# Weight loads issued from GpSimd, ScalarE's stores from ScalarE, and GpSimd's arithmetic on other engines

## The chip, the cores and the metric

The kernel runs on one core of a Trainium2 chip, as one launch. The metric is the device time of that launch in microseconds, the median of several runs. A core has a matrix engine (TensorE, PE), a vector engine (VectorE, DVE), an activation engine (ScalarE, ACT), a general engine (GpSimd, POOL) and a queue engine (SyncE, SP). Each has its own instruction stream and works in order; semaphores tie the streams together. A DMA is issued by an instruction in one of these streams: if that instruction must wait, everything behind it in the stream waits too.

## The reference

A trunk of two layers over 512 latent tokens and 256 context tokens, 1024 channels, one batch entry, all in float32. Cut to what matters:

```python
for l in range(DEPTH):                                   # DEPTH = 2
    mod = silu(c) @ w_mod[l] + b_mod[l]                  # shifts, scales, gates; the same for the context
    h = modulate(rmsnorm(x, g0), shift1, scale1)
    s5, q, k, v, hq, hff, hfb, hi, hg, gate = split_columns(h @ w_in[l])
    ya = s5_branch(s5)                    # bidirectional diagonal state space model, then a GLU
    yb = windowed_attention(rope(q), rope(k), v)         # window 128, context keys, sink logits
    yc = hgrn2_branch(hq, hff, hfb, hi, hg)              # gated linear recurrence, both directions
    m = sum(sigmoid(gate_b) * (y_b @ w_branch[b]) for b, y_b in enumerate((ya, yb, yc)))
    x = x + g1 * rmsnorm(m @ w_out[l], g1n)
    h = modulate(rmsnorm(x, g2n), shift2, scale2)
    a, g = split(depthwise_conv(h @ w_up[l]))
    x = x + g2 * rmsnorm((silu(a) * g) @ w_down[l], g3n)
# the context stream goes through the same layer, except in the last; the latent stream is returned
```

## The kernel before

**Weights.** Channels lie on partitions and tokens along the free axis (tiles of 128x768: 256 context and 512 latent columns). Every weight tile of 128x1024 is split into a high and a low part. `wload` (L286) loads it into a raw buffer `wr` (three buffers), ScalarE rounds it to `wh`, VectorE subtracts to get `wl`; `product` (L312) then makes three matmuls per 128 channels (high by high, high by low, low by high). The results go to PSUM in `mm` (512 columns, two buffers) and `mc` (256 columns, one buffer), and ScalarE or VectorE evacuates them. `hold` (L335) does the same with weights that stay in SBUF for a while, as the down projection does.

**Stages.** A layer runs: norm and `s5_in` (L1421, the s5 branch's columns of `w_in`, evacuated by ScalarE and stored to DRAM in eight stores `ud` a tile); attention (`att_in` L1018 with its rotary helper `rope`, `attention` L1065, whose result goes to `yb`); `hgrn` (L1280) with its input `hg_in` (L1231, which stores the output gate `tgd`), woven with `gates` (L854, which stores the branch gates `gd`) and with set-up work; `s5` (L1715, with `stage_a` and `stage_b`, which stores `yd`), `merge`, `w_out`, `residual` (L584), `ffn` (L732). The norms' last step is `norm_part` (L552): TensorE transposes pieces into PSUM (`pa`), ScalarE applies scale and shift, GpSimd makes the rounded high part and VectorE the low part.

**Set-up work.** `mods_rows` (L418) makes modulation vectors from loads of `in_wmodt` by VectorE; `s5_prep` (L1655) makes the s5 branch's matrices and passes them through DRAM: `mid`, `bbd`, `cad` in, `mt` (stored from a tile that ScalarE wrote), `kd` and `tod` out. `stage_a` loads `mt`, `tod`, `cad` and `phd` back.

**Order.** A scheduler that builds the program decides the order of each engine's instructions by priorities: weight loads are raised (`high_priority`), set-up is lowered. Scratch tiles come from one pool of 52 slots, so a tile's name says little: `slot` may be any of them. All DMAs are SyncE's. DMAs of SyncE and ScalarE take turns on eight completion counters (`DMAHW0` to `DMAHW7` in the rows of the order), and each waits for the one eight before it; GpSimd's have eight of their own (`DMASW0` to `DMASW7`). Every instruction is recorded through one helper, so each row of the profile names L121: tiles tell the rows apart.

## Time and profile before

| | us |
|---|---|
| median of three runs (lowest, highest) | 2694.89 (2693.42, 2697.78) |
| the profiled execution | 2701.07 |
| its span, first to last instruction | 2699.3 |
| TensorE's matmuls busy | 2536.5 |
| VectorE, ScalarE, GpSimd busy | 1896.8, 1021.7, 121.0 |

The mean granted clock of TensorE over the span is 0.975 of full speed. Times of the profile are from one execution and start at its first instruction. A row of a timeline gives the start, the length and the instructions that follow each other alike (x4), and in brackets the engine's idle time before them and what ended it; SPq is SyncE as a queue, where the length is that of issuing. A releaser is inferred from semaphores: the last thing that the instruction waited for.

### The profile page before, as it was taken

What the parts mean: (1) busy time and instruction counts of PE and PEld (TensorE: products, weight loads), DVE (VectorE), ACT (ScalarE), POOL (GpSimd) and SP (SyncE); (2) the same over time, 40 slices, a digit from 0 to 9 for tenths busy, and PEclk for the clock granted to TensorE, in tenths of its full rate; (3) what the DMA queues carried; (4) which work ended last, traced back from release to release, by engine and by line L of the source; (5) the groups of instructions that cost most, each with busy time, mean ns of one, the idle gap of its engine ahead of it and who ended that gap; (6) DMA issues with size and microseconds to landing.
All of it is one profiled execution on the core that took longest, in us unless ns stands there. A gap on an engine that the chain in (4) does not pass through costs nothing. (4 is left out here: it accounts for less than half of the span.)

```text
span 2699.3 us, 47069 instructions
## 1 busy us (share of the span) xinstructions
PE 2536.5 (94%) x18436; PEld 2129.6 (79%) x18436; DVE 1896.8 (70%) x4304; ACT 1021.7 (38%) x1813; POOL 121.0 (4%) x182
## 2 busy tenths in 40 slices
PE   5999998899989999999999989899999989999998
PEld 3876776687878898887888878667787778888887
DVE  6799483778576659999974566754767856666656
ACT  3356522221223345442433463562222334443334
POOL 1100000001000010000000011000000000100000
PEclk8999999999989999999999999999999989999999
DMA  7443545453566344534434557422334565333332
GB/s 246 129 127 118 166 146 164 156 165 99 169 210 213 119 128 145 162 108 131 123 102 123 155 180 222 130 82 93 107 116 131 170 213 167 110 121 112 96 100 96
DMA packets 243214, 381.36 MB, mean 141 GB/s; under 512 B 54032, under 2 KB 139440, under 8 KB 242992
## 3 DMA queue, kind: packets, MB, share of 16 engines
q1 hardware_dynamic: 242992, 378.36, 44.8%
q8 instruction: 145, 2.38, 0.4%
q14 instruction: 77, 0.63, 0.1%
HBM read 301.26 MB, written 81.21 MB: 142 GB/s over the span
## 5 line engine op out<-in xcount | busy, mean ns | idle before, releaser
L121 PE MATMUL mm<-slot,wh 128*128 128x512 f32 (+1 forms) x3798 | 1200.3, 394 | 23.5 <-DVE slot L121 9.4
L121 PEld LDWEIGHTS mm<-slot,wh 128*128 128x128 f32 x3798 | 699.8, 190 | 160.9 <-DVE slot L121 13.4
L121 PE MATMUL mm<-slot,wl 128*128 128x512 f32 (+1 forms) x1899 | 742.3, 391 | 2.7 <-issue 1.9
L121 DVE TENSOR_TENSOR slot<-slot,slot 128x384 f32<-128x384 f32 (+17 forms) x1340 | 666.3, 535 | 101.5 <-ACT slot L121 59.3
L121 PE MATMUL mc<-slot,wh 128*128 128x256 f32 (+1 forms) x3082 | 666.7, 309 | 9.4 <-ACT slot L121 7.3
L121 PEld LDWEIGHTS mc<-slot,wh 128*128 128x128 f32 x3082 | 518.8, 193 | 57.2 <-ACT slot L121 10.8
L121 DVE TENSOR_TENSOR wl<-wr,wh 128x1024 fp32r<-128x1024 f32 (+1 forms) x274 | 333.8, 1219 | 239.3 <-ACT wh L121 235.1
L121 ACT ACTIVATE wh<-wr 128x1024 fp32r<-128x1024 f32 (+1 forms) x274 | 288.5, 1053 | 531.3 <-PE mc L121 373.0
L121 PE MATMUL mc<-slot,wl 128*128 128x256 f32 (+1 forms) x1541 | 474.6, 308 | 0.0
L121 PEld LDWEIGHTS mm<-slot,wl 128*128 128x128 f32 x1899 | 359.9, 190 | 72.8 <-DVE wl L121 1.6
L121 PEld LDWEIGHTS pa<-slot,slot 128*32 128x32 f32 (+2 forms) x5696 | 213.2, 133 | 126.5 <-issue 62.3
L121 PE MATMUL pa<-slot,slot 128*32 128x32 f32 (+8 forms) x5696 | 254.8, 227 | 57.8 <-DVE slot L121 26.5
L121 PEld LDWEIGHTS mc<-slot,wl 128*128 128x128 f32 x1541 | 296.7, 193 | 14.1 <-issue 1.2
L121 ACT ACTIVATE slot<-slot 128x768 fp32r<-128x768 f32 (+5 forms) x253 | 168.3, 669 | 367.8 <-DVE slot L121 307.7
L121 ACT ACTIVATE slot<-mm 128x512 f32<-128x512 f32 (+1 forms) x180 | 103.6, 576 | 320.7 <-PE mm L121 299.5
L121 DVE CUSTOM_DVE_ANT_0 mscr<-slot,slot 128x768 bf16<-128x768 f32 (+1 forms) x256 | 178.2, 696 | 41.0 <-DMA slot<-in_wmodt 37.5
L121 ACT ACTIVATE slot<-pa 128x512 f32<-128x512 f32 (+7 forms) x250 | 115.3, 493 | 231.0 <-PE pa L121 189.8
L121 PE MATMUL pa<-cst,slot 128*128 128x128 f32 x900 | 139.5, 286 | 23.8 <-DVE slot L121 13.2
L121 PEld LDWEIGHTS pa<-cst,slot 128*128 128x128 f32 x900 | 107.4, 145 | 53.2 <-ACT slot L121 23.4
L121 PE MATMUL mm<-slot,slot 128*128 128x256 f32 (+1 forms) x784 | 111.1, 319 | 17.4 <-DMA slot<-in_wmod 15.6
L121 DVE SCALAR_TENSOR_TENSOR slot<-slot,slot 128x256 f32<-128x256 f32 (+7 forms) x129 | 92.3, 722 | 41.0 <-ACT slot L121 40.3
L121 PEld LDWEIGHTS mm<-slot,slot 128*128 128x128 f32 (+1 forms) x784 | 93.1, 185 | 22.6 <-issue 17.9
(160 smaller groups left out, 1521.9 us busy)
## 6 DMA issues: line engine op xcount, KB each, us to landing
wr<-in_win SPq DMA_DIRECT2D x108, 512.0 KB
wr<-in_wup SPq DMA_DIRECT2D x88, 512.0 KB
slot<-in_wmodt SPq DMA_DIRECT2D x80, 384.0 KB
wr<-in_wdn SPq DMA_DIRECT2D x32, 512.0 KB
slot<-cad SPq DMA_DIRECT2D x48, 256.0 KB
wr<-in_wbr SPq DMA_DIRECT2D x24, 512.0 KB
slot<-in_wmodt SPq DMA_DIRECT2D x80, 128.0 KB
cad<-slot SPq DMA_DIRECT2D x64, 144.0 KB
```

Source lines behind the costliest of these rows:

```text
L121: return _f(*(x.ap if isinstance(x, Slot) else x for x in a), **{k: x.ap if isinstance(x, Slot) else x for k, x in kw.items()})
```

## The change

The 288 weight loads of `wload` and `hold` are issued by GpSimd. The 162 stores of tiles that ScalarE has just written (`gd` 48, `yb` 10, `tgd` 8, `ud` 64, `mt` 32) are issued by ScalarE. The other 935 DMAs stay with SyncE. GpSimd computes nothing: in `norm_part` ScalarE writes the high part from PSUM itself, and VectorE computes the unrounded value from PSUM once more and subtracts; the rotary product goes to VectorE, the gate's key `k` to ScalarE, the memsets to VectorE, and the scan mask is one ScalarE copy of a broadcast.

```diff
         with self.tc.high_priority(offset=self.whp):
-            nc.sync.dma_start(raw[:, :n], src)
+            nc.gpsimd.dma_start(raw[:, :n], src)
...
             with self.tc.high_priority(offset=self.whp):
-                nc.sync.dma_start(raw[:, :P * n], src)
+                nc.gpsimd.dma_start(raw[:, :P * n], src)
...
-                nc.scalar.activation(h[:, tk], pt[:, n * i:n * i + n], AF.Identity,
-                                     bias=self.mod[l][:, 8 * sh + k, tt:tt + 1],
-                                     scale=self.amod[l][:, j, k, tt:tt + 1])
-                nc.gpsimd.tensor_scalar(hh[:, tk], h[:, tk], 1.0, 0.0, ALU.mult, ALU.add)
+                a, b = self.amod[l][:, j, k, tt:tt + 1], self.mod[l][:, 8 * sh + k, tt:tt + 1]
+                nc.scalar.activation(hh[:, tk], pt[:, n * i:n * i + n], AF.Identity, bias=b, scale=a)
+                nc.vector.tensor_scalar(h[:, tk], pt[:, n * i:n * i + n], a, b, ALU.mult, ALU.add)
                 nc.vector.tensor_sub(hl[:, tk], h[:, tk], hh[:, tk].bitcast(F32))
...
-                nc.sync.dma_start(d[:, t0:], tg[:, t0:])
+                nc.scalar.dma_start(d[:, t0:], tg[:, t0:])
...
-            nc.gpsimd.tensor_mul(s[:, 256:], s[:, 256:], sin)
+            nc.vector.tensor_mul(s[:, 256:], s[:, 256:], sin)
...
-            nc.gpsimd.tensor_scalar(k, th, self.hgn[:, c:c + 1], self.hgc[:, c:c + 1], ALU.mult, ALU.add)
+            nc.scalar.activation(k, th, AF.Identity, bias=self.hgc[:, c:c + 1], scale=self.hgn[:, c:c + 1])
...
-                nc.sync.dma_start(d[16 * j:16 * j + 16].rearrange("c g k -> g c k"), u[:, 96 * j:96 * j + 96])
+                nc.scalar.dma_start(d[16 * j:16 * j + 16].rearrange("c g k -> g c k"), u[:, 96 * j:96 * j + 96])
...
-            nc.gpsimd.memset(bb, 0.0)
+            nc.vector.memset(bb, 0.0)
...
-            nc.gpsimd.memset(mz, 1.0)
-            nc.gpsimd.tensor_mul(m3, m3, m8k[:, x0:x0 + 4].unsqueeze(2).to_broadcast([P, 4, 96]))
-            nc.gpsimd.memset(m3[:, :, 0:1], 0.0)
+            nc.scalar.activation(m3, m8k[:, x0:x0 + 4].unsqueeze(2).to_broadcast([P, 4, 96]), AF.Copy)
+            v.memset(m3[:, :, 0:1], 0.0)
```

The other stores of the list change in the same way, and one more memset goes to VectorE.

The scheduler moves much with it. Three places, first SyncE while the first layer's `hgrn` runs with set-up behind it; before, with `wr` the weights' raw buffers:

```order
L121 DMA slot_764_4679<-mid_1225 128x512
L121 DMA mt_4672<-slot_766_4686 128x512
L121 DMA mt_4672<-slot_768_4694 128x512
L121 DMA tod_4663<-kd_4366 8x16x128 x3
L121 DMA wr_5901<-in_win 128x1024
L121 DMA tod_4663<-kd_4366 8x16x128
L121 DMA wr_6110<-in_win 128x1024
L121 DMA tod_4663<-kd_4366 8x16x128 x4
L121 DMA slot_769_4697<-in_wmodt 128x768
L121 DMA slot_771_4705<-in_wmodt 128x768
```

and in the change:

```order
L121 DMA slot_764_4679<-mid_1225 128x512
L121 DMA slot_769_4697<-in_wmodt 128x768
L121 DMA tod_4663<-kd_4366 8x16x128 x8
L121 DMA slot_771_4705<-in_wmodt 128x768
L121 DMA slot_770_4704<-in_wmodt 128x256
L121 DMA slot_772_4712<-in_wmodt 128x768
L121 DMA slot_770_4704<-in_wmodt 128x256
L121 DMA slot_800_5009<-bbd_1231 128x2x128
L121 DMA slot_809_5044<-in_wmodt 128x768
```

The weight loads are gone, the `tod` stores stand in one piece, and an `in_wmodt` load stands ahead of them. Second SyncE in the first layer's `s5` stage, before (`mt` is loaded for the next products, `yd` is stored for the merge):

```order
L121 DMA yd_8432<-slot_1189_8426 16x8x96
L121 DMA wr_9046<-in_wglu 128x1024
L121 DMA yd_8432<-slot_1189_8426 16x8x96 x7
L121 DMA gd_8500<-slot_1196_8497 128x768
L121 DMA slot_1198_8502<-mt_5333 128x768
L121 DMA slot_1199_8504<-mt_5333 128x256
L121 DMA slot_1200_8506<-phd_1230 128x768
```

and in the change (`slot_1198` and `slot_1199` are the same two loads of `mt`):

```order
L121 DMA slot_1198_8496<-mt_5333 128x768
L121 DMA slot_1207_8544<-yd_1397 128x768
L121 DMA slot_1185_8390<-mt_5333 128x256
L121 DMA slot_1186_8392<-phd_1230 128x768
L121 DMA slot_1210_8550<-yd_1397 128x768
L121 DMA yd_7965<-slot_1127_7959 16x8x96 x8
L121 DMA slot_1183_8386<-ud_853 128x768
L121 DMA slot_1199_8498<-mt_5333 128x256
L121 DMA slot_1200_8500<-phd_1230 128x768
```

Both `mt` loads now stand ahead of the eight `yd` stores of the same tile, which follow eleven rows below (`yd_8426`), though the second stands behind the stores of the tile before; no weight load is near. Third ScalarE in the first layer's `s5_in`, before (`mm` and `mc` are evacuations from PSUM):

```order
L121 ACTIVATE slot_140_550<-mm_500 128x8x64
L121 ACTIVATE wh_795<-wr_794 128x1024
L121 ACTIVATE slot_140_550<-mc_501 128x8x32
L121 ACTIVATE slot_166_690<-mm_640 128x8x64
L121 ACTIVATE wh_877<-wr_876 128x1024
L121 ACTIVATE slot_166_690<-mc_641 128x8x32
L121 ACTIVATE slot_178_776<-mm_726 128x8x64
```

and in the change, with what each instruction waits for in brackets:

```order
L121 ACTIVATE slot_140_550<-mc_501 128x8x32 [waits PE_49]
L121 DMA ud_553<-slot_140_550 8x16x96 [waits DMAHW2_49,Activation_49]
L121 DMA ud_553<-slot_140_550 8x16x96 [waits DMAHW4_49]
L121 DMA ud_553<-slot_140_550 8x16x96 [waits DMAHW5_49]
L121 DMA ud_553<-slot_140_550 8x16x96 [waits DMAHW6_49]
L121 DMA ud_553<-slot_140_550 8x16x96
L121 DMA ud_553<-slot_140_550 8x16x96 [waits DMAHW0_49]
L121 ACTIVATE wh_877<-wr_876 128x1024 [waits DMASW4_49,PE_49]
L121 DMA ud_553<-slot_140_550 8x16x96 [waits DMAHW3_49]
L121 DMA ud_553<-slot_140_550 8x16x96 [waits DMAHW4_49]
L121 ACTIVATE slot_166_690<-mc_641 128x8x32 [waits PE_49]
```

The `ud` stores stand between the evacuations, and several wait for a counter that a DMA of SyncE used last.

## Rows read from the trace of the kernel before

**Rows 1.** The page: engines, DMA queue, one group (busy, mean ns | idle before).
```profile
PE 2536.5 (94%) x18436; PEld 2129.6 (79%) x18436; DVE 1896.8 (70%) x4304; ACT 1021.7 (38%) x1813; POOL 121.0 (4%) x182
...
q1 hardware_dynamic: 242992, 378.36, 44.8%
...
L121 PEld LDWEIGHTS mm<-slot,wl 128*128 128x128 f32 x1899 | 359.9, 190 | 72.8 <-DVE wl L121 1.6
```

**Rows 2.** The waits of SyncE's queue: us in total, times, longest.
```profile
SPq L121 <- DVE wl L121: 813.4, 204, 13.8
SPq L121 <- DVE slot L121: 578.0, 232, 16.2
```

**Rows 3.** The waits of all engines, same columns.
```profile
ACT wh L121 <- PE mc L121: 373.0, 142, 8.0
```

**Rows 4.** The timeline of VectorE, then TensorE, at the first gap.
```profile
463.79 0.96 DVE L121 CUSTOM_DVE_ANT_0 mscr<-slot,slot 128x768 bf16<-128x768 f32 x1 [6.74 <-DMA slot<-in_wmodt]
...
467.15 1.51 PE L121 MATMUL pa<-slot,slot 128*32 128x32 f32 x96 [8.91 <-DVE slot L121]
```

**Rows 5.** The timeline of SyncE's DMA issues before that gap.
```profile
441.63 1.97 SPq L121 DMA_DIRECT2D tod<-kd  x3
451.31 0.34 SPq L121 DMA_DIRECT2D wr<-in_win  x1
451.69 0.62 SPq L121 DMA_DIRECT2D tod<-kd  x1
457.08 0.34 SPq L121 DMA_DIRECT2D wr<-in_win  x1
...
460.18 2.52 SPq L121 DMA_DIRECT2D slot<-in_wmodt  x5
```

**Rows 6.** The timeline of TensorE at the second gap.
```profile
784.21 2.15 PE L121 MATMUL pa<-slot,slot 128*64 128x96 f32 x23 [9.93 <-DMA slot<-mt]
```

**Rows 7.** The timeline of SyncE's DMA issues before the second gap.
```profile
768.81 0.32 SPq L121 DMA_DIRECT2D yd<-slot  x1
775.12 0.35 SPq L121 DMA_DIRECT2D wr<-in_wglu  x1
775.51 3.28 SPq L121 DMA_DIRECT2D yd<-slot  x7
...
779.38 0.96 SPq L121 DMA_DIRECT2D slot<-mt  x2
```

**Rows 8.** Windows: length; PE, PEld, DVE, ACT, POOL; PEclk, DMA share, GB/s.
```profile
778.00:792.00 14.00, 7.15 (x44) 6.24 (x45) 10.15 (x18) 4.03 (x8) 1.46 (x4) 0.51 1.01 331
460.00:478.00 18.00, 9.09 (x224) 7.10 (x225) 11.77 (x28) 2.23 (x6) 0.00 (x0) 0.53 0.98 319
...
20.00:40.00 20.00, 14.46 (x95) 6.30 (x93) 16.83 (x108) 5.38 (x9) 3.30 (x4) 1.00 1.00 359
```

**Rows 9.** The timeline of the start: SyncE, then TensorE.
```profile
35.00 1.00 SPq L121 DMA_DIRECT2D wr<-in_win  x2
...
50.99 1.19 PE L121 MATMUL mm<-slot,wh 128*128 128x512 f32 x2 [6.72 <-issue]
```

**Rows 10.** The timeline of SyncE in the first layer's s5 input.
```profile
90.36 3.65 SPq L121 DMA_DIRECT2D ud<-slot  x6
```

**Rows 11.** The timeline of ScalarE in the same stretch.
```profile
92.81 0.60 ACT L121 ACTIVATE slot<-mm 128x512 f32<-128x512 f32 x1 [4.27 <-PE mm L121]
95.51 1.06 ACT L121 ACTIVATE wh<-wr 128x1024 fp32r<-128x1024 f32 x1 [2.10 <-PE mc L121]
```

**Rows 12.** GpSimd's groups by shape: busy us, mean ns | idle before.
```profile
L121 POOL TENSOR_SCALAR slot<-slot 128x256 fp32r<-128x256 f32 x72 | 39.0, 563 | 495.7 <-ACT slot L121 494.1 <-PE mm L121 1.2
...
L121 POOL TENSOR_TENSOR slot<-slot,slot 128x512 f32<-128x512 f32 x10 | 17.0, 1704 | 139.0 <-DVE slot L121 65.6 <-DMA slot<-in_sin 40.9 <-issue 32.4
```

**Rows 13.** Two of VectorE's groups by shape, same columns.
```profile
L121 DVE TENSOR_TENSOR slot<-slot,slot 128x256 fp32r<-128x256 f32 x72 | 35.4, 540 | 11.9 <-POOL slot L121 11.9
...
L121 DVE TENSOR_TENSOR slot<-slot,mc 128x256 f32<-128x256 f32 x32 | 13.4, 418 | 9.9 <-PE mc L121 9.8
```

More of the change, by code (lines that the diff above doesn't have):

```diff
@@ L1152, in values @@
             nc.scalar.activation(yt, po, AF.Copy)
-            nc.sync.dma_start(yb[:, :, P * n:P * n + P], yt.rearrange("p (i q) -> p i q", i=4))
+            nc.scalar.dma_start(yb[:, :, P * n:P * n + P], yt.rearrange("p (i q) -> p i q", i=4))
             yield
@@ L1249, in hg_in @@
         tgd = self.dr.tile([P, NT], F32, name=self.nm("tgd"))
-        nc.sync.dma_start(tgd[:, t0:], z[:, t0:])
+        nc.scalar.dma_start(tgd[:, t0:], z[:, t0:])
         yield
@@ L1675, in s5_prep @@
                     nc.scalar.activation(tr[:, :512], pt[:, P * i:P * i + 512], AF.Copy)
-                    nc.sync.dma_start(mt[:, i0 + i:i0 + i + 4, :], tr[:, :512].rearrange("p (g k) -> p g k", k=P))
+                    nc.scalar.dma_start(mt[:, i0 + i:i0 + i + 4, :], tr[:, :512].rearrange("p (g k) -> p g k", k=P))
                 yield
@@ L1804, in stage_a @@
             st = 0 if d == 0 else 31
-            nc.gpsimd.memset(hcat.rearrange("p (g c) -> p g c", c=96)[:, :, st:st + 1], 0.0)
+            v.memset(hcat.rearrange("p (g c) -> p g c", c=96)[:, :, st:st + 1], 0.0)
             for g2 in range(2):
```

## The prediction

> **What bounds the kernel now.** The page's first part comes first: TensorE's matmuls cover 94% of the span, VectorE 70%, ScalarE 38%, GpSimd 4%, and one hardware queue, SyncE's, carries all the data [rows 1]. So a microsecond is won only where TensorE stands idle or runs at its lower clock. The idle time between its matmuls, added up over the trace, is about 156 us, 33 of it before 100 us, and most of the rest lies in a dozen gaps. Second the waits, SyncE's own among them: its queue stood 813 us before instructions that VectorE's `wl` released. Those are weight loads waiting for a raw buffer, and whatever stood behind them waited too; another 578 us went to slots that VectorE still held [rows 2]. Third, who suffers: hardly the weights. TensorE's waits for `wl` come to 1.6 us [rows 1], while ScalarE, about to copy the next weight, stood 373 us waiting for TensorE, 142 times, 2.6 us each [rows 3]: weights are ready ahead of need. The held queue hurts where something else stands in it, and two places show that.
>
> At 458 us TensorE stops for 8.91 us on a tile of VectorE, which itself idled 6.74 us for a load of `in_wmodt` [rows 4]. That load issued at 460.18; before it SyncE stood from 443.60 to 451.31 and from 452.31 to 457.08 at weight loads [rows 5]. At 774 us TensorE stops for 9.93 us on a load of `mt` [rows 6]; SyncE stood from 769.13 to 775.12 at a `wglu` load, then issued seven `yd` stores in 3.28 us, and the `mt` loads left at 779.38 [rows 7]. Around both gaps the granted clock is 0.53 and 0.51 [rows 8], nearly the lower level (1.2 GHz): the gap costs more than its length.
>
> **The change part by part**, against the profiled execution (2701.1 us, 6 us above the median of 2694.9; the terms are carried over to the median unchanged).
>
> (a) *Weights leave SyncE, gap at 458.* In the order of the change no weight load stands near the `tod` stores and the first `in_wmodt` load moves ahead of them. SyncE's two holds were 7.7 + 4.8 = 12.5 us, more than the gap, so the wait for the load is over before TensorE needs its tile. The gap is worth 8.9. In 467 to 478 TensorE worked near the lower clock; at full clock its 11 us would take about 6, so up to 5 more. I take 2 of the 5, since other waits stand close behind it there: −11, between −14 and 0 (0 if VectorE's own queue is late next).
>
> (b) *Gap at 774.* Without the `wglu` load the `yd` stores and the `mt` loads leave 775.12 − 769.13 = 6.0 us sooner; in the order of the change the two `mt` loads even stand ahead of those stores, the second behind those of the tile before, and the gap may close wholly. −6 for the hold, −2 of the clock: −8, between −14 (9.9 and the clock's 4) and 0. The other stretches in which SyncE was held ended on no long gap: −1, between −6 and 0.
>
> (c) *Weights on GpSimd's queue.* 288 loads of up to 512 KB, in order among themselves and behind nothing else, since GpSimd computes nothing. No row shows a DMA issued there; the nearest is SyncE's issue of the same load, 0.34 us [rows 5]. I take it at nothing: the cover is the weights' lead. It is gone if a load comes later than the products of a tile take, about 8 us in the s5 input (see (e)). Upper bound in the rivals.
>
> (d) *The start.* Three weight loads now go out first, ahead of `x` and `in_wmod`: 3 × 0.52 MB at 359 GB/s is 4.4 us in a stretch whose DMA share is 1.00 [rows 8]. Against it: in before the first two left at 35.00, and TensorE waited 6.72 us until 50.99 [rows 9], part of it for the copy of that weight. Bounds +5 and −6; I take 0, as both act on one chain.
>
> (e) *Stores on ScalarE.* 162 of them: 64 `ud` at 3.65/6 = 0.61 us [rows 10] is 39 us; the other 98, priced between a plain load's 0.34 and 0.61, 33 to 60 us. In the s5 input, where they are densest, ScalarE waits 4.27 and 2.10 us for TensorE in each tile of about 8 us (with 0.60 and 1.06 of work and the second evacuation); eight `ud` issues are 4.9 us, so they fit into 6.4 with 1.5 to spare [rows 11]. But ScalarE works in order, and what is queued behind a store is the next PSUM evacuation, for which TensorE waits (`mc` has one buffer). SyncE's and ScalarE's DMAs take turns on eight completion counters, each waiting for the one eight before; in the built program 110 of the 162 stores wait for a SyncE transfer this way, which may itself wait for VectorE. Lower bound 0, all hidden; upper bound: every fourth of the 110 outlasts the mean 2.6 us of slack by 1 us, 27 us. I take +5, near the lower end, by the s5 row, the only one that shows a full tile.
>
> (f) *GpSimd's arithmetic.* The norm: 72 pieces of 128x256 at 563 ns leave GpSimd [rows 12]; ScalarE's evacuation now writes the high part directly, and VectorE adds one piece from PSUM, at 418 ns by its nearest row of that size, to a subtraction that took 540 beside GpSimd and should take about 420 alone [rows 13]. So the first high part comes 0.56 us sooner, and the eighth low part 8 × (0.84 − 0.56) = 2.2 us later. There are nine such groups; with all on the path +20, with TensorE fed by other work 0. TensorE takes the pieces one by one and mostly has other tiles there: +3. The ten rotary products took 1.7 us each on GpSimd [rows 12] and about 0.7 on VectorE, which in the first layer's attention is already busy; the shorter chain roughly pays for the load: −2, between −6 and +4. The gate product and the masks go to ScalarE and the memsets to VectorE in stretches where both have idle time: 0, with ScalarE busy 38% of the span; if one of the 32 ScalarE operations this adds came ahead of an evacuation, it would cost its own length, under 1 us, and stands in (e)'s range.
>
> Sum: −11 − 8 − 1 + 0 + 0 + 5 + 3 − 2 = **−14**, so 2694.9 − 14 = **2681 us**.
>
> A rule that speaks against (a) and (b): the holds in [rows 2] are waits of the head of a queue, not issue time. The Trainium skill, "DMA: Bandwidth & Descriptors", section "Issuing engines are not separate DMA queues", says that DMAs started by several engines run on the same 16 engines, and that starting them from more than one saves only the sequencer's time to initiate each. By that rule alone (a) and (b) would be 0 and the sum about +5; the trace disagrees in so far as SyncE stood idle at 444 to 457 before a load whose buffer was not free, while later ones could go.
>
> **The rivals.** *No change, about 2692.* The same transfers are no longer held, but the stage waits for something else: the 578 us at VectorE's slots stay on SyncE [rows 2], and where TensorE stops for an operation of VectorE, that may be late for its own reasons. If two thirds of (a) and (b) are refilled, the sum is −14 + 13 = −1, with (b)'s small rest −3: 2692. For it: VectorE at 70%. Against: at 458 VectorE idled.
>
> *Slower, about 2712: ScalarE stalls at its stores.* Its place is the stages in which SyncE runs set-up work of VectorE's while ScalarE evacuates `mm` and `mc`: the hgrn and s5 stages and the second layer's s5 input, where `ud` stores stand among `in_wmodt` loads. A store that waits on a SyncE counter holds the evacuation behind it. Its price is (e)'s upper 27 us, and with some of (a) refilled (+4) the sum is −14 + 22 + 4 = +12, up to +17: 2707 to 2712. It decides from some 20 stalls that outlast the slack by 1 us. For it: 110 such waits. Against: the counters' earlier transfers were issued eight DMAs ago, and SyncE is less held than before.
>
> *Slower: weights late.* If a load on GpSimd's queue takes so long that it outlasts the lead, every tile pays: 0.1 us on each of 288 is 29 us, 2710 with the gains kept. For it: no row shows this queue. Against: the lead, and a queue in which weights stand behind nothing. The Trainium skill, "SBUF — State Buffer", section "SBUF: two separate sides", says that descriptors of GpSimd's DMAs are written by GpSimd itself, and that VectorE's two-port operations lock it out meanwhile. By it loads would be slowest where VectorE is fullest; no row here can show that.
>
> **How the numbers follow.** A measurement can tell about 0.2%, 5.4 us, so "same" is 2689.5 to 2700.3. The forecast case has 0.60, of which some 0.50 lies below 2689.5 and 0.10 within; no change 0.15, of which 0.05 falls below and 0.10 within; ScalarE's stalls 0.15 and late weights 0.10, all but 0.02 of them slower. Faster 0.56, same 0.21, slower 0.23. The low end takes (a), (b) and (d) at their best with the rest as summed: −14 − 3 − 6 − 6 = −29, and a little for (e) at 0: 2660. The high end reaches the stalls, 2712; beyond it stand late weights that cost more.
>
> **What would show it.** Right: SyncE's waits for `wl` vanish; the gaps at 458 and 774 close or end on another releaser; TensorE's waits for `wl` stay near 2 us; ScalarE's waits for matmuls shrink by some 75 to 100 us, the issue time. Wrong: gaps that end on ScalarE just behind a store; a wait of `wh` for the weight's DMA that comes back in every tile; new gaps after the norms that end on VectorE's low parts; or both gaps gone and the span unmoved, which would say that the work was late anyway.

## The result, and the profile after

The changed kernel takes 2711.25 us (median of 5 runs, 2707.54 to 2715.45), the kernel before 2694.89 beside it (5 runs, 2691.98 to 2699.49): a ratio of 1.006, 95% interval 1.0043 to 1.0077. It is **slower, by 16 us**. The prediction said 2681, faster: the sign is wrong, while the range (2660 to 2712) just holds the time. The profiled execution took 2711.25 us, with a span of 2709.5.

First the page of the changed kernel, the lines that answer to [rows 1], and GpSimd's one group.

```profile
PE 2543.7 (94%) x18436; PEld 2131.7 (79%) x18436; DVE 1913.0 (71%) x4434; ACT 1048.4 (39%) x1845; POOL 152.5 (6%) x292
...
q1 hardware_dynamic: 174864, 196.93, 23.4%
q0 software_dynamic: 40448, 148.92, 18.0%
q10 hardware_dynamic: 26656, 32.51, 3.4%
...
L121 PEld LDWEIGHTS mm<-slot,wl 128*128 128x128 f32 x1899 | 361.9, 191 | 73.9 <-issue 3.3
...
L121 POOL DMA_DIRECT2D wr<-in_win x108 | 57.1, 529 | 1220.9 <-DVE wl L121 959.4
```

There are three queues now: q0 is GpSimd's, with 149 MB of weights, q10 ScalarE's, with 33 MB of stores. TensorE is busy 7 us longer. Now the waits, of the queues, of ScalarE and of TensorE's weight loads, answering to [rows 2], [rows 3] and [rows 1].

```profile
POOL wr L121 <- DVE wl L121: 2174.5, 252, 82.2
...
SPq L121 <- DVE slot L121: 1036.1, 218, 51.7
...
ACT wh L121 <- PE mc L121: 325.3, 138, 8.3
ACT slot L121 <- DMA ud<-slot: 25.2, 6, 10.2
ACT wh L121 <- DMA ud<-slot: 22.8, 4, 9.1
...
ACT wh L121 <- DMA wr<-in_win: 16.0, 6, 6.0
...
PEld mm L121 <- DVE wl L121: 0.8, 1, 0.8
```

The wait for a raw buffer moved where it was meant to go: GpSimd stands 2174 us in it, and SyncE has no row of that kind left (813.4 in [rows 2]). ScalarE waits 48 us less for TensorE, and 48 us for its own `ud` stores, which is new. TensorE's weight loads wait 0.8 us for `wl`, before 1.6: hardly a weight is late for TensorE. ScalarE does wait longer for weights that are still being loaded, 36.9 us in all in place of 18.6, but in 6 of the 108 `in_win` tiles and not in every one.

The gap at 458 us is gone. SyncE's issues and TensorE's matmuls at that place:

```profile
445.04 5.19 SPq L121 DMA_DIRECT2D tod<-kd  x8
450.28 13.52 SPq L121 DMA_DIRECT2D slot<-in_wmodt  x4
```
```profile
450.93 1.05 PE L121 MATMUL pa<-slot,slot 128*32 128x32 f32 x96 [0.29 <-DVE slot L121]
```

SyncE goes straight from the `tod` stores to the `in_wmodt` loads, with one such load ahead of the stores as well, and the same 96 matmuls that had waited 8.91 us [rows 4] wait 0.29. In the windows of [rows 8] the granted clock is full again at the first place; at the second it is between the levels (1.2 and 2.4 GHz), so a gap remains there.

```profile
460.00:478.00 18.00, 18.00 (x281) 14.19 (x280) 12.61 (x30) 4.85 (x9) 1.05 (x2) 1.00 0.61 184
778.00:792.00 14.00, 8.93 (x49) 8.04 (x47) 12.04 (x26) 3.26 (x4) 0.53 (x1) 0.76 0.46 150
```

Where the time went is told by a table of progress. It is worked out from the traces: the time at which TensorE reaches its n-th product with a weight's low part (3456 of them; their order differs a little between the kernels, but not in how many of each kind stand before the n shown here), minus that of before. The letters stand for the kernels of the experiments: W weights alone, S stores alone, A arithmetic alone, AW both of these without the stores; a 9 behind them means nine set-up buffers.

```
     n  before us   change      W      S      A     AW    AW9     A9  change9
     0       53.1     -2.4   -0.3    0.2   -2.7   -2.9   -2.9   -2.4     -1.9
   256      264.5     16.8   13.9   11.4    5.6   13.7    5.7    5.9      9.0
   512      480.8      3.2    2.4    7.6   -7.6   -9.2  -16.4   -4.4     -8.7
   896      813.3    -13.4   -3.5    1.7  -11.7   -9.4  -16.6   -8.6    -23.4
  1536     1190.3     -9.5   -0.9    2.0   -9.8   -5.8  -12.5   -6.8    -19.4
  1920     1398.3      4.7    9.9    3.2   -6.1   10.2  -10.1   -4.9    -17.2
  2176     1544.5     20.4   22.3   11.3   -6.3   24.3   -5.0   -4.5      0.2
  2304     1666.9     32.9   15.8   18.8    3.4   26.4   -4.8    2.6      7.9
  2816     2204.6      7.8    3.9    7.1  -12.7    7.2  -29.9  -14.9    -18.1
   end     2699.3     10.2    4.7    7.0  -12.4    7.2  -26.5  -15.6    -16.8
```

The change loses 19 us by 264, in the first layer's s5 input and attention, makes good for them by 813, and at 1190 us is ahead by 9.5. It then loses 14 us by 1398, in the first layer's feed-forward with the second layer's set-up running behind it, 16 more by 1544, in the rest of that feed-forward, 12 more by 1667, in the second layer's s5 input (the arithmetic alone loses 10 there), and regains 25 by 2204. So the question was what is late from 1190 on.

### The profile page after: what moved, and what is told of

Its sections match the earlier page's. It is cut to its first block, busy times and chain, and to the rows that moved or that the text cites. A ratio compares the mean times of both kernels' runs of the same rounds, so it can differ in the third digit from the quotient of the medians.

```text
span 2709.5 us, 47040 instructions
## 1 busy us (share of the span) xinstructions
PE 2543.7 (94%) x18436; PEld 2131.7 (79%) x18436; DVE 1913.0 (71%) x4434; ACT 1048.4 (39%) x1845; POOL 152.5 (6%) x292
## 5 line engine op out<-in xcount | busy, mean ns | idle before, releaser
L121 DVE TENSOR_TENSOR slot<-slot,slot 128x384 f32<-128x384 f32 (+13 forms) x1350 | 653.4, 521 | 103.6 <-ACT slot L121 60.4
L121 PE MATMUL mc<-slot,wh 128*128 128x256 f32 (+1 forms) x3082 | 670.1, 310 | 25.4 <-DVE slot L121 13.6
L121 PE MATMUL pa<-slot,slot 128*32 128x32 f32 (+8 forms) x5696 | 251.4, 226 | 38.2 <-issue 13.6
L121 PE MATMUL mm<-slot,slot 128*128 128x256 f32 (+1 forms) x784 | 112.9, 323 | 21.7 <-DVE rs_v L121 18.6
L121 POOL DMA_DIRECT2D wr<-in_win x108 | 57.1, 529 | 1220.9 <-DVE wl L121 959.4
```

The costliest lines, as they stand in the source:

```text
L121: return _f(*(x.ap if isinstance(x, Slot) else x for x in a), **{k: x.ap if isinstance(x, Slot) else x for k, x in kw.items()})
```

## The experiments

Each kernel is compared with the kernel before on the same chip. The explanations weighed are the prediction's rivals (ScalarE stalls at its stores; weights late), that the scheduler's other order is to blame whatever was moved, and, once the first traces were there, that VectorE waits for set-up buffers whose stores are still under way.

### The three parts apart

Weights alone:

```diff
-            nc.sync.dma_start(raw[:, :n], src)
+            nc.gpsimd.dma_start(raw[:, :n], src)
...
-                nc.sync.dma_start(raw[:, :P * n], src)
+                nc.gpsimd.dma_start(raw[:, :P * n], src)
```

> The kernel before with one part of the change: the 288 weight loads issued by GpSimd, in order with its arithmetic, which stays. Theory A (the two long gaps of SyncE's hold were a true gain, the loss comes from the other two parts): 2675 to 2685, the gaps at 458 and 774 gone or under 5 us. Rival B (taking the weights away from SyncE lets set-up transfers run ahead, and that itself makes the losses after 1200 us): 2700 to 2715, with new gaps between 1230 and 1510 us. Rival C (a GpSimd-issued load is late): TensorE or ScalarE's wh waits for wr in many tiles, over 30 us in all.

Stores alone, five lines of this kind (`gd`, `yb`, `tgd`, `ud`, `mt`):

```diff
-                nc.sync.dma_start(d[16 * j:16 * j + 16].rearrange("c g k -> g c k"), u[:, 96 * j:96 * j + 96])
+                nc.scalar.dma_start(d[16 * j:16 * j + 16].rearrange("c g k -> g c k"), u[:, 96 * j:96 * j + 96])
```

> The kernel before with one part of the change: the 162 stores of tiles that ScalarE wrote are issued by ScalarE; weights stay on SyncE. Theory A (a store on ScalarE waits behind a SyncE transfer on its completion counter and holds the evacuation): 2700 to 2720, ScalarE waits of 5 us and more that end on ud stores in layer 1's s5 input, as in the change (10.18, 5.07, 9.06 us there). Rival B (the stalls come only when SyncE, free of weights, has many in_wmodt loads under way): 2690 to 2700, no such waits over 3 us.

GpSimd's arithmetic alone, the other hunks of the change:

```diff
-                nc.gpsimd.tensor_scalar(hh[:, tk], h[:, tk], 1.0, 0.0, ALU.mult, ALU.add)
...
+                nc.vector.tensor_scalar(h[:, tk], pt[:, n * i:n * i + n], a, b, ALU.mult, ALU.add)
...
-            nc.gpsimd.tensor_mul(s[:, 256:], s[:, 256:], sin)
+            nc.vector.tensor_mul(s[:, 256:], s[:, 256:], sin)
```

> The kernel before with one part of the change: GpSimd computes nothing; all DMAs stay on SyncE. Theory A (VectorE's added work costs where VectorE is full, 1000 to 1300 us, and in the norms): 2700 to 2710, VectorE's groups up by 15 to 20 us, wider gaps near 1240 and in the norms near 1615. Rival B (the added work is hidden, and the loss in that stretch is due to the order that the other parts bring): 2690 to 2698.

Measured: weights 2708.5 us (1.0041, 1.0029 to 1.0053), so **+12**; stores 2705.15 (1.0031, 1.0019 to 1.0043), **+8.5**; arithmetic 2684.93 (0.9957, 0.9943 to 0.9971), **−11.7**. Their sum is +8.7, the change +16.4. The part that was to bring the gain costs the most, and the one priced at +1 brings 12; it came out faster than either range that was expected of it.

Weights alone keep the gain at 458 us, and show why there is none at 774. The last `mt` load before it on SyncE, then TensorE there, weights alone, then TensorE in the whole change:

```profile
758.01 1.21 SPq L121 DMA_DIRECT2D slot<-mt  x1
```
```profile
791.75 0.80 PE L121 MATMUL mm<-slot,wh 128*128 128x512 f32 x1 [11.60 <-DVE slot L121]
```
```profile
786.35 3.94 PE L121 MATMUL pa<-slot,slot 128*128 128x96 f32 x16 [5.07 <-DVE slot L121]
```

The loads of `mt`, which ended the 9.93 us of [rows 6], now go out by 758 and are no longer the releaser; an operation of VectorE, which works without a pause from 777 to 792, ends a gap that is as long. In the whole change other work fills part of it.

Stores alone show the stall of the rival. The first layer's s5 input, issues and evacuations on ScalarE, then TensorE:

```profile
75.03 6.11 ACTq L121 DMA_DIRECT2D ud<-slot  x8
...
101.02 8.92 ACTq L121 DMA_DIRECT2D ud<-slot  x8
110.05 0.60 ACT L121 ACTIVATE slot<-mm 128x512 f32<-128x512 f32 x1 [9.36 <-DMA ud<-slot]
```
```profile
111.92 0.50 PE L121 MATMUL mc<-slot,wh 128*128 128x256 f32 x2 [2.02 <-ACT slot L121]
```

Eight stores hold ScalarE for 6.1 to 8.9 us, not the 4.9 of the prediction; the evacuation behind them is late, and TensorE stands 2 us for it. At the 128th product (130 us) stores alone are 8.7 us behind. It is not the issuing that takes longer. All `ud` issues, minimum, median and longest in ns, on SyncE in the kernel before, then on ScalarE with stores alone:

```profile
L121 SPq DMA_DIRECT2D ud<-slot x64: 570/570/779, 74.6 to 1667.2; - x64
```
```profile
L121 ACTq DMA_DIRECT2D ud<-slot x64: 579/590/2067, 75.0 to 1679.7; - x64
```

The rest is waiting between the issues. Worked out from the completions, the 8.92 us are 4.7 of issuing and 4.0 of three waits for completion counters that SyncE's stores of `mid` and `cad` had used last. That is the mechanism of the prediction's second rival.

### Two closer cuts: the rotary product, and ud of the second layer

```diff
-            nc.gpsimd.tensor_mul(s[:, 256:], s[:, 256:], sin)
+            nc.vector.tensor_mul(s[:, 256:], s[:, 256:], sin)
```

> The kernel before with one line of the change: the ten rotary products go from GpSimd to VectorE. Theory A (the arithmetic's gain of 12 us is this product, whose 1.6 us on GpSimd stood in the chain to the first scores; the gap of 6.66 us at 152 is what went): 2684 to 2689, the gap at 152 under 3 us and the progress from 180 us on about 9 us ahead. Rival B (the gain is spread over the norms, masks and keys): 2692 to 2697.

Measured: 2689.25 us against 2696.54 (0.997, 0.996 to 0.9981), −7.3: this single line makes some six tenths of the arithmetic's gain. The gap that it shortens, in the first layer's attention, in the kernel before and with this line alone:

```profile
159.04 0.79 PE L121 MATMUL pa<-slot,slot 128*128 128x256 f32 x2 [6.66 <-ACT slot L121]
```
```profile
154.58 0.63 PE L121 MATMUL pa<-slot,slot 128*128 128x256 f32 x2 [2.30 <-ACT slot L121]
```

TensorE stood 6.66 us for the chain of shuffle, product and rounding before, and a product 1 us shorter, with no hop to another engine and back, takes 4.4 of it at this place. The line also changed VectorE's order there; how the 4.4 divide between the two was not separated.

The change, with the second layer's `ud` stores back on SyncE:

```diff
-                nc.scalar.dma_start(d[16 * j:16 * j + 16].rearrange("c g k -> g c k"), u[:, 96 * j:96 * j + 96])
+                (nc.scalar if l == 0 else nc.sync).dma_start(d[16 * j:16 * j + 16].rearrange("c g k -> g c k"), u[:, 96 * j:96 * j + 96])
```

> The change with one part undone: the 32 ud stores of layer 1 go back to SyncE. Theory A (ScalarE's stalls at these stores, 24 us of waits, cost about 13 us of TensorE's progress between 1655 and 1700): 2696 to 2702, no wait of ScalarE for a ud store in layer 1, the progress against the kernel before no worse at 1700 than at 1560. Rival B (the stall is given back in layer 1's attention, where TensorE waits for others anyway): 2706 to 2713. Rival C (on SyncE the stores now stand behind the in_wmodt loads, and the s5 branch or attention waits for them): over 2713.

Measured: 2706.67 us (1.0038, 1.0026 to 1.005). That is 10.0 above the kernel before beside it, where the change is 16.4 above its own: some 6 us less, though the two intervals overlap, and short of the 2702 that theory A asked for. What the changed kernel's trace shows at this place follows: SyncE, first its waits from 1660 to 1710 us, then ScalarE with its issues, and TensorE.

```profile
SPq L121 <- DVE macc L121: 15.3, 11, 3.5
SPq L121 <- DMA ud<-slot: 15.1, 8, 3.7
```
```profile
1664.54 43.78 SPq L121 DMA_DIRECT2D slot<-in_wmodt  x22
```
```profile
1671.02 6.75 ACTq L121 DMA_DIRECT2D ud<-slot  x10
1677.82 0.38 ACT L121 ACTIVATE slot<-mc 128x256 f32<-128x256 f32 x1 [10.18 <-DMA ud<-slot]
...
1685.46 8.91 ACTq L121 DMA_DIRECT2D ud<-slot  x7
1694.49 1.06 ACT L121 ACTIVATE wh<-wr 128x1024 fp32r<-128x1024 f32 x1 [9.06 <-DMA ud<-slot]
```
```profile
1678.26 0.73 PE L121 MATMUL mc<-slot,wh 128*128 128x256 f32 x2 [5.00 <-ACT slot L121]
```

SyncE issues 22 `in_wmodt` loads in 44 us, held by VectorE's `macc` and, just as long, by ScalarE's `ud` stores through the counters that the two engines share. ScalarE issues its stores in long rows, the evacuation `slot<-mc` starts 10.18 us after ScalarE's last operation, and TensorE stands 5 us. The place and the victim are those of the prediction's second rival; the holder is not. Worked out from the completions, ScalarE stood 12.0 us in the whole change before `ud` stores whose counter was not free: 11.6 of them for an earlier `ud` store of its own, and 0.4 for a transfer of SyncE, which the rival had named (6.8 and 7.9 with stores alone). And it is 5 or 6 us of 16.

### Weights: the queue, or the order?

The change without the stores:

```diff
-                nc.scalar.dma_start(d[16 * j:16 * j + 16].rearrange("c g k -> g c k"), u[:, 96 * j:96 * j + 96])
+                nc.sync.dma_start(d[16 * j:16 * j + 16].rearrange("c g k -> g c k"), u[:, 96 * j:96 * j + 96])
```

> The change without its stores part: weights on GpSimd, which computes nothing; all stores on SyncE. Theory A (the parts add up: weights +12, arithmetic -12): 2693 to 2700. Rival B (weights lose only because they stand behind GpSimd's arithmetic, which is gone here): 2675 to 2685. Rival C (the parts make each other worse, VectorE's load and the set-up work ahead of it): over 2704.

The same with only the weights of the mixing half on GpSimd; those of the feed-forward's loops stay on SyncE:

```diff
-            nc.sync.dma_start(raw[:, :n], src)
+            (nc.gpsimd if mix else nc.sync).dma_start(raw[:, :n], src)
...
-                    w = self.wload(I["wup"][l, 2 * i + g])
+                    w = self.wload(I["wup"][l, 2 * i + g], mix=False)
```

> The arithmetic part of the change, and of the weight loads those of the mixing half (w_in, w_branch, w_glu, w_out) on GpSimd; the feed-forward's w_up and the w_down loads inside its loop stay on SyncE. Theory A (weights off SyncE gain in the hgrn and s5 stages and lose in the feed-forward, where set-up work of VectorE then stands ahead of the convolutions): 2668 to 2680, no new loss between 1200 and 1560 us, the gaps near 455 and 765 shorter than with the arithmetic alone. Rival B (weights on GpSimd lose everywhere, by their landing or their place): 2690 to 2700. Rival C (it is the order's luck): anywhere from 2675 to 2700, with gains and losses in other places than A names.

And a control that moves no queue and no operation, only the order, by one number of the planner's table:

```diff
-WV = {... "fs": 22, ...}
+WV = {... "fs": 23, ...}
```

> The kernel before with a number of its planner moved by a hair: the rate at which set-up work is handed to the scheduler behind layer 0's feed-forward, 22 to 23. No engine, queue or operation changes; only the order of some instructions does, by about as many lines as with the weights' move. Theory A (the order is tuned so finely that any such shift costs or gains 5 to 10 us): a distance of over 5 us from the kernel before either way. Rival B (the order's shift alone is worth little, and the losses come from the queues): within 4 us of the kernel before.

Measured: without the stores 2708.87 us against 2696.54 (1.0036, 1.0022 to 1.005): weights on top of the arithmetic cost 24 us. With the feed-forward's weights back on SyncE 2692.28 (0.9979, 0.9969 to 0.999): 16.6 of the 24 go with these loads (and with six of the sixteen `w_out` loads, which pass through `hold` as well and went back with them). The other 7 stay, and the time lies in rival B's range. The control 2700.15 (1.0015, 1.0006 to 1.0025), which is +3.6. It moves the order less than weights alone do: in the traces VectorE's sequence of operations differs from that of before by 432 lines, with weights alone by 930. So it does not rule out that a new order makes a larger part of the 24; it does show that a difference of 3 or 4 us between two kernels of different order is no proof of a cause.

What this part of the feed-forward (1180 to 1400 us) has with all weights on GpSimd and hardly otherwise is a wait of VectorE for a DMA. Its rows there, us in total, times, longest: arithmetic alone, then without the stores, then the whole change; the kernel before has none.

```profile
DVE slot L121 <- DMA mid<-slot: 1.6, 3, 1.1
...
DVE slot L121 <- DMA phd<-slot: 0.3, 1, 0.3
```
```profile
DVE slot L121 <- DMA mid<-slot: 5.1, 3, 1.7
DVE slot L121 <- DMA cad<-slot: 4.0, 4, 2.8
DVE slot L121 <- DMA phd<-slot: 1.9, 1, 1.9
```
```profile
DVE slot L121 <- DMA mid<-slot: 5.3, 3, 1.9
DVE slot L121 <- DMA cad<-slot: 3.1, 3, 2.3
DVE slot L121 <- DMA phd<-slot: 2.1, 1, 2.1
```

`cad`, `mid` and `phd` are the DRAM tiles that the second layer's set-up writes; `DMA mid<-slot` is a store from a buffer, and VectorE waits for its end before it writes that buffer again. The set-up has seven buffers (`ASIDE = 7`). The totals are 0 before, 1.9 with the arithmetic, 1.5 with the mixing half, 1.3 in the control, 8.5 with weights alone, 11.0 without the stores and 10.5 in the change. The last three lose 11 to 16 us between 1190 and 1398 us, counted as in the table, the others 6 at most. Next, how such a wait reaches TensorE. VectorE and TensorE with the arithmetic alone:

```profile
1232.68 0.76 DVE L121 TENSOR_TENSOR slot<-slot,slot 128x576 f32<-128x576 f32 x1 [1.11 <-DMA mid<-slot]
...
1245.22 0.68 DVE L121 TENSOR_TENSOR slot<-slot,mm 128x512 f32<-128x512 f32 x1
```
```profile
1245.96 0.79 PE L121 MATMUL mm<-slot,wh 128*128 128x512 f32 x1 [3.96 <-DVE slot L121]
```

and the same operations without the stores (arithmetic and weights):

```profile
1237.54 1.43 DVE L121 TENSOR_TENSOR slot<-slot,slot 128x576 f32<-128x576 f32 x2 [1.70 <-DMA mid<-slot]
...
1251.15 0.68 DVE L121 TENSOR_TENSOR slot<-slot,mm 128x512 f32<-128x512 f32 x1
```
```profile
1251.88 0.80 PE L121 MATMUL mm<-slot,wh 128*128 128x512 f32 x1 [9.96 <-DVE slot L121]
```

VectorE has no idle time between its wait and the operation that empties the PSUM tile (`slot<-slot,mm`); whatever it lost before reaches TensorE, which comes to a stop at 1242.0 in both kernels and stands 9.96 us in place of 3.96. Between 1184 and 1376 us VectorE's own lag in the second kernel behind the first, taken at its `wl` subtractions, grows from 4.0 to 16.3 us, 12.3 in all, of which the extra waits are 9.1.

### The test: nine set-up buffers

If that is the cause, two more buffers mend it, and mend it only where weights have left SyncE. The edit takes away what makes VectorE wait, the same one line in four kernels: arithmetic and weights, arithmetic alone (the control), the whole change, and the whole change with all 64 `ud` stores back on SyncE.

```diff
-ASIDE = 7
+ASIDE = 9
```

> The change without its stores part (e4_weights_arith, 2708.9), with nine set-up buffers in place of seven in layer 0 (ASIDE), so that VectorE rewrites a set-up tile two tiles later. Theory A (with weights on their own queue VectorE stands at tiles whose stores cad, mid and phd are still under way, 11 us between 1180 and 1400, and loses there what TensorE then waits for): these waits under 3 us, the loss between 1200 and 1400 us from 20 to under 8, 2690 to 2698. Rival B (the weights' queue costs in another way, by landing or by the order): the waits fall and the time stays at 2703 or above. Rival C (two buffers fewer for the main work cost as much as they give): the loss moves to the mixing half, 2700 to 2712.

> The control: the arithmetic part alone (e3_arith, 2684.9), all DMAs on SyncE, with nine set-up buffers in place of seven. Theory A: VectorE hardly waited for these stores there (1.9 us between 1180 and 1400), so nothing is gained: 2682 to 2688. Rival C (fewer buffers for the main work): 2690 or above. Rival D (more buffers help any variant): under 2680, and then e10_aside9 tells nothing of the weights' queue.

> The whole change with nine set-up buffers instead of seven: e10_aside9 plus its stores part. Theory A (the set-up buffers were the main loss, the stores on ScalarE a second one of 2 to 9 us): 2685 to 2694, ScalarE's waits that end on ud stores over 30 us. Rival B (with the buffers mended the stores cost nothing): 2679 to 2684. Rival C (the buffers help only without the stores): 2700 or above.

> The same with the 64 ud stores back on SyncE; gd, yb, tgd and mt stay on ScalarE. Theory A (of the stores only ud hurts, since eight in a row stand before an evacuation): 3 to 9 us under e12, 2674 to 2684, no ScalarE wait for a ud store. Rival B (the other 98 stores hurt as much): within 3 us of e12. Rival C (ud on SyncE delays the in_wmodt loads behind them in layer 1): above e12.

| kernel | seven buffers | nine buffers | ratio with nine (95%) |
|---|---|---|---|
| arithmetic | 2684.93 | 2682.53 | 0.9943 (0.9921 to 0.9966) |
| arithmetic, weights | 2708.87 | 2683.22 | 0.9946 (0.9926 to 0.9967) |
| whole change | 2711.25 | 2686.37 | 0.9958 (0.9943 to 0.9974) |
| whole change, `ud` on SyncE | not run | 2682.89 | 0.9946 (0.9932 to 0.9961) |

The two buffers are worth 25.7 us with weights on GpSimd, 24.9 in the whole change and 2.4 in the control (26.3, 28.1 and 3.0 with each kernel taken against the kernel before beside it). The first came out better than theory A's range, the other three within it. VectorE's waits for set-up stores from 1180 to 1400 us are what is left of 11.0 with nine buffers (arithmetic and weights):

```profile
DVE slot L121 <- DMA mid<-slot: 0.2, 1, 0.2
```

The same wait stands at the start of the first layer, with arithmetic and weights from 100 to 340 us:

```profile
DVE slot L121 <- DMA mid<-slot: 5.7, 4, 2.0
DVE slot L121 <- DMA cad<-slot: 1.2, 3, 0.6
DVE slot L121 <- DMA phd<-slot: 0.4, 1, 0.4
```

With the arithmetic alone and with nine buffers there is none of it, and at 264 us the three stand at 13.7, 5.6 and 5.7 in the table. The kernel with only the mixing half's weights on GpSimd has 6.0 us of it there and, counted the same way, stands at 12.4. Of the 33.6 us between the two profiled runs of arithmetic and weights, seven and nine buffers, 8 are there by 264 us, 13.6 come between 1190 and 1398, and 9 from there to 1544.

That **shows the cause**: the change is slower because VectorE, where it is full (busy for 202 of the 220 us from 1180 on, with the arithmetic alone), waits for set-up buffers whose stores are under way. One reservation stays: nine buffers change the order, too. In the control they do so nearly as much (868 differing lines of VectorE's sequence against 1132) and bring 3. The test also shows what was not lost: with nine buffers weights on GpSimd cost 0.7 us (2683.22 against 2682.53), which is nothing that can be told. Nor do they gain anything: the kernel that only moves the arithmetic off GpSimd and leaves every DMA on SyncE is as fast as any. The `ud` stores on ScalarE cost 3.5 us (2686.37 against 2682.89), near what the closer cut gave, though of the size of the order's control. In the profiled run with nine buffers and the stores back, ScalarE has no wait for `ud` left; the whole change with nine buffers had 45.6 us of them.

### What stays open

Why the stores are under way longer was not separated. Worked out from the completions in the traces, a store of `cad`, `mid` or `phd` beside a weight load between 1180 and 1400 us lands in 2.8 to 3.0 us on average where the feed-forward's weights are on SyncE, and in 3.1 to 3.4 where they are on GpSimd (2.2 to 2.5 with no weight load near). The longest is 4.2 us before, but 5.7 with the arithmetic alone, and 5.5 to 6.3 with weights on GpSimd. But the scheduler also moves one or two of VectorE's rewrites of these buffers ahead, by the built order, of which no view is shown here. Either gives such waits. No run holds the order and moves the queue.

The 16 us that the whole change loses from 1398 to 1544 us it loses with nine buffers too (17, from −17.2 to 0.2 in the table), and arithmetic and weights with nine lose 5; most of it is regained by 2204. A trace of it is there in the change, TensorE's waits from 1400 to 1560 us:

```profile
PE pa L121 <- DMA slot<-cad: 6.7, 2, 3.9
PE pa L121 <- DMA slot<-mid: 1.1, 1, 1.1
```

Together they are 7.8 us, 6.3 in the change with nine buffers, 2.3 with the arithmetic alone, which loses nothing there, and 0 in arithmetic and weights with nine. No edit tried whether that is the cause. Last, the −26.5 at the end of that column comes from a profiled run of 2674.58 us, the shortest of its kernel, whose median is 2683.22: for what a change is worth the medians count, the table only for where.

## Why the prediction was wrong

The step that failed is (c), which put the move of the weights at nothing; (b) and (f) were mis-sized beside it. That the time falls inside the range is luck: the upper end was priced by ScalarE's stalls, which are some 4 of the 16 us.

**(a), gap at 458: right.** Weights alone gain 11.5 us between 421 and 548 us of before (from 6.5 behind to 5.0 ahead), forecast −11. The granted clock is full where it was 0.53. By the Trainium skill, "DMA: Bandwidth & Descriptors", section "Issuing engines are not separate DMA queues", which the prediction weighed, this would have been 0, and at this place the trace disagrees: a wait at a queue's head does hold what stands behind it. Over the whole kernel, with the buffers mended, the measurement agrees with it: more than one queue 2682.89 to 2686.37, one queue 2682.53. In the profiled runs with nine buffers, weights on top of the arithmetic are 12 us ahead at 481 us (−16.4 against −4.4) and 0.5 at 1544, though that run, the shortest of its kernel, is ahead again later.

**(b), gap at 774: wrong, −8 forecast, −0.8 measured** between 751 and 813 us with weights alone (−5.5 in the whole change, where other work fills part of the gap). The hold and the wait for `mt` went as described, but VectorE ends a gap of 11.6 us. The prediction had named this end of the range ("if VectorE's own queue is late next") for (a) only, and chose the gap's length by the hold that ended last. A releaser that comes last hides those that come just before it.

**(c), weights on GpSimd: the step that failed, 0 forecast, +24 measured.** "I take it at nothing: the cover is the weights' lead" held for what it looked at. The weights are not late for TensorE, as forecast; the third rival falls. But the part's cost was looked for in the weights alone. What was to be asked is who shares the DMA engines and the schedule with them: the stores of the set-up, whose buffers VectorE rewrites with no slack at the start and from 1180 to 1400 us. It made 24 us of the 28 between the arithmetic alone and the change, each against its own before (2684.93, then 2708.87 with the weights, then 2711.25). No row of before shows the wait from 1180 on; from 100 to 340 us of before there were 3.1 us of it, which the prediction does not use, and which are the hint that seven buffers are only just enough.

**(d), the start: right**, 0 forecast and −2.4 at the first product; in the kernel with weights alone it is −0.3, so it comes from the arithmetic.

**(e), stores on ScalarE: right in the main, +5 forecast, +8.5 measured alone**, 3.5 (all `ud`, nine buffers) and some 6 (the second layer's) beside the rest. Eight `ud` issues cost what the sum had, 4.7 us against 4.9. What was put too low is the waits between them, up to 4.0 us in a tile, where the slack left 1.5. The prediction counted ScalarE's waits for SyncE's transfers. The two other kinds were left out: ScalarE's waits for its own earlier stores (11.6 us in the change), and SyncE's waits for ScalarE's stores (15.1 us at one place). The place in the second layer was the second rival's.

**(f), GpSimd's arithmetic: mis-sized, +1 forecast, −11.7 measured.** The rotary product alone is −7.3 (forecast −2): that it stands on a chain for which TensorE waited 6.66 us was in the trace of before, and the prediction does not use it. For the norm, VectorE's two groups in the changed kernel:

```profile
L121 DVE TENSOR_SCALAR slot<-pa,amod,mod 128x256 f32<-128x256 f32 x72 | 38.1, 542 | 9.6 <-ACT slot L121 8.6 <-PE mm L121 0.9
L121 DVE TENSOR_TENSOR slot<-slot,slot 128x256 fp32r<-128x256 f32 x72 | 29.3, 422 | 0.4
```

The subtraction fell from 540 ns [rows 13] to 422, as forecast, but the new pass over PSUM takes 542 and not 418, so the last low part of a group of eight comes 8 × (0.96 − 0.56) = 3.2 us later and not 2.2. Yet what is left of the part's gain after the rotary product is −4.4, not +3. Which edit brings it was not split.

**The signs to look for**: SyncE's waits for `wl` vanished, the first gap closed, the second ended on another releaser, TensorE's weight loads waited 0.8 us for `wl`, and ScalarE's waits for matmuls shrank by 48 us in place of 75 to 100; the other 48 it spent waiting at its own stores. One sign fits the result, "gaps that end on ScalarE just behind a store"; the sign that mattered, VectorE waiting for a store, was not on the list. One reading of before was off as well: of the 123 us that TensorE idled after 100 us, the twelve longest gaps hold 57, and not most.

Put together by the runs: −12 for the arithmetic, +24 for weights with seven buffers, +4 for the stores (2708.87 and 2711.25, each against its own before), sum +16. With nine buffers it is −15, +1 and +2, sum −12, which is 2686.37, near the 2681 forecast; but the gain in it is another one, from the arithmetic, and not from the queues.

## What to carry to other kernels

Before a queue is split, look for buffers with only just enough copies whose stores travel beside the stream that is moved: any wait of a full engine for a store of its own result, however small, marks them, and one more buffer is cheaper than the loss. Take a gap as won only if the second-last to arrive there is early, too. And weigh the humble part of a change by the chain on which it stands: one product taken off a slow helper engine was worth more than three queues.

## What the runs showed of the hardware that was not expected

- A DMA issue takes 0.53 us of GpSimd for a weight (page of after, 529 ns), against 0.34 us of SyncE for the same load [rows 5]. Worked out from the completions, the medians from issue to landing are 4.1 us for `in_win` and 3.8 for `in_wup` from GpSimd, and 3.8 and 3.6 from SyncE in the kernel before.
- The Trainium skill, "SBUF — State Buffer", section "SBUF: two separate sides", says that GpSimd cannot write its DMAs' descriptors while VectorE runs a two-port operation; the prediction drew from it that loads would be slowest where VectorE is fullest. The trace of the change does not show that: of its loads of `in_win`, `in_wup` and `in_wdn`, those with VectorE busy for over 90% of their time took 3.88 us as a median (82 loads), those with it busy for under half 3.86 (81). Which of VectorE's operations are of that kind, no row tells.
- A `ud` store costs ScalarE 0.59 us to issue as a median, and SyncE 0.57. DMAs of the two engines that share completion counters hold each other both ways: 4.0 us of ScalarE's waits for SyncE's stores in one row of eight (stores alone), 15.1 us of SyncE's waits for ScalarE's stores in 50 us (the change).
- VectorE took 542 ns for a 128x256 scale and bias out of PSUM, and 418 ns for an addition that reads PSUM at the same size [rows 13].
